# Softmax weights of 20 attention heads turned by VectorE and through DRAM instead of by TensorE

## The chip, the cores and the metric

One NeuronCore of a Trainium2 chip runs the whole program. The time is the device time of one execution in microseconds (us). The kernel before was timed in three runs: 898.75, 900.03 and 900.44 us, median 900.03 us.

## The reference, cut to what matters

A two-layer causal decoder trunk over 256 tokens of width 2048, in fp32. Each layer is a norm, one wide input projection, two kinds of attention heads, a SiLU gate, an output projection and the residual; a last norm follows.

```python
for i in range(DEPTH):                    # DEPTH = 2
    x = layer_even(x, norm0, w_in0, w_out0) if i % 2 == 0 else layer_odd(x, norm1, w_in1, b_f1, w_out1)
return rmsnorm(x, norm_f)
# layer_even: 10 heads "A" (an indexer picks 64 keys a query), 6 heads "B" (dilated windows)
# layer_odd:   8 heads "C" (stick-breaking, no softmax),        8 heads "D" (softmax with forget gates)
p = jax.nn.softmax(logits, axis=-1)       # A, B and D
o = jnp.einsum('bhqk,bkhd->bqhd', p, v)   # y = o * silu(gate); x + y @ w_out
```

## The kernel before, in words

**The projections.** TensorE's work is a chain of jobs (`jobs`, line 229): 14 of the first input projection (B0, K, I0, I1, B1, B2, B3, five pairs of A heads, B4, B5), four of its output projection (P0 to P3), 17 of layer two (C0, F1, G1, C2 to C7, D0 to D7) and four of the last output projection (Q0 to Q3). A job multiplies the 256 tokens (two tiles of 128) by a block of weights, mostly 512 columns wide, in 16 steps of 128 rows: *K steps*. Weights and activations are split into a high and a low fp32r part, so a K step is six matmuls (`products`, lines 320 to 326). F1 and G1 share the work of head C1 and are only 264 and 256 columns wide: the *narrow* jobs.

**The weights' way.** A weight *piece* is four K steps (1 MB for 512 columns). SyncE's queue (SP) issues its load into one of three `raw` tiles (`load`, line 256). ScalarE copies it in two halves to `whi` (line 282), VectorE subtracts to get `wlo` (line 283). Both have four buffers; `split` runs three halves ahead of the matmuls. A load overwrites the tile of the piece three before it, so SP waits for that piece's `wlo`.

**The order.** Every engine works through its instructions in the order in which the program writes them. `tick` (line 307) counts one tick for each K step of 512 columns (half a tick for a narrow one). Work beside the projections stands in generators: `yield n` puts what follows n ticks further on. A job is thus 16 ticks. When all of a piece is split, `split` starts `later(load, 4)` (line 287): the next load is issued four ticks on.

**A softmax head.** After its projection, `softmax_head` (line 540; heads B and D) or `heads_a` (line 723; two A heads) has queries and keys turned, multiplies them (`soft`, line 512: matmuls into `s`, exponentials into the tile `sn`, 128 x 384: 128 weights for the first 128 tokens and 256 for the second) and scales the weights (`share`, line 535). Then the weights must be turned, since the product with the values needs keys on partitions. `turn` (line 397) does this with three 128 x 128 TensorE transposes (line 400) into the PSUM tile `tp`; `cut` (line 465) reads `tp` into high and low parts; `weigh_out` (line 498) or its counterpart in `heads_a` multiplies by the values (`o`).

**The other way of turning** is in use already for queries, keys and gates (`qk`, `u`). `grid` (line 420) is one VectorE STREAM_TRANSPOSE, which turns each 32 x 32 block on its own into a tile `far`. `moved` (line 431) stores `far` to DRAM (`fard`, line 436) and reads it back so that the blocks land on their new partitions (line 438). What arrives is in block order with its rows permuted by `FAR` (line 52), and the host permutes the gate's weight columns to suit. Both transfers stand in SP's queue among the weight loads, and the reading waits until the store has landed. Gate values are turned this way by `gate_turned` (line 487), starting four ticks after the head.

Of the kernel before, what the change touches and what calls it, by code (L numbers as in the profile page):

```python
# [174 lines left out]
def trunk(ctx, tc, x, xT, g1, w0, wo0, w1, wo1, bf, gf, consts, rope, out):  # L175
# [243 lines left out]

    def grid(srcs):  # L420

        t = hp.tile([P, 512], F32, name="far", tag="rt2")
# [64 lines left out]
    def gate_turned(u, n=NT):  # L487
        uT = hp.tile([P, P * n], F32, name="uT", tag="uT" if n == NT else "rl")
        start(far([u], uT, 4, 2, 4))
        return arrived(uT, n)  # L490

    def gate_turned_here(u):
        pt = turn([u[:, 0:P], u[:, P:SEQ]])
        uT = hp.tile([P, SEQ], F32, name="uT", tag="uT")
        nc.scalar.activation(uT, pt[:, 0:SEQ], AF.Copy)
        return quarters(uT)

    def weigh_out(ph, pl, p1, v, uT, kt, swap):

        vh, vl, v1 = v  # L500
# [38 lines left out]

    def softmax_head(qk, ticks, nb, v, u, rs, kt, last):  # L540
        uT = None if last else gate_turned(u)
# [73 lines left out]
    def head_b(ps, h):  # L615
# [16 lines left out]
        if not last:  # L632
            start(far([qk], qk, 2, 2, 4))
        yield from softmax_head(qk, 12, bmask, v, u, hr0, YPOS[f"B{h}"], last)

# [22 lines left out]
    def index(ps, c):  # L658
        qr = [hp.tile([P, 512], F32, name="iqr", tag="qk") for _ in range(NT)]

        ih = hp.tile([P, 2, 512], F32R, name="ih", tag="ih", bufs=1)
        il = hp.tile([P, 4, 2, P], F32R, name="il", tag="il", bufs=1)
        for th in range(NT):
# [3 lines left out]
        yield 12  # L667
        hi, lo = (quarters(ih[:, j]) for j in range(2))
        nc.scalar.activation(hi, arrived(qr[0], 4), AF.Copy)
# [3 lines left out]
        d = [slice(0, DI), slice(DI, P)]  # L673
        two = lambda j: il[:, :, j].rearrange("p a (i c) -> p a i c", i=4)
        for j in range(2):
# [4 lines left out]
        for h2 in range(4):  # L680
            for th, s in BLK:
                n = P * (th + 1)
                pS = pa.tile([P, 512], F32, name="s", tag="s", bufs=1)
                if th == 0:
                    a = slice(h2 * P, (h2 + 1) * P)
                    three(pS[:, 0:SEQ], ih[:, 0, a], ih[:, 1, a], ikh[:, SEQ:512], ikl[:, SEQ:512])
                else:
                    for j in range(2):
                        o = pS[:, j * SEQ:(j + 1) * SEQ]
                        nc.tensor.matmul(o, il[:, h2, j], ikh[:, 0:SEQ], start=True, stop=False)  # L690
                        nc.tensor.matmul(o, il[:, h2, j], ikl[:, 0:SEQ], start=False, stop=True)
                rl = hp.tile([P, 512], F32, name="rl", tag="rl")
# [30 lines left out]
    def heads_a(ps, h):  # L723
# [22 lines left out]
        js = [slice(j * P, (j + 1) * P) for j in range(2)]  # L746

        ph, pl = (hp.tile([P, 2, SEQ], F32R, name="pA" + n, tag="i" + n, bufs=1) for n in "hl")
        p1h, p1l = (hp.tile([P, 2 * P], F32R, name="pB" + n, tag=t, bufs=1) for n, t in (("h", "y"), ("l", "sp")))

        def turned(j, pr):
            pt = turn([pr[:, 0:P], pr[:, P:SEQ], pr[:, SEQ:384]])
            cut((ph[:, j, :], pl[:, j, :]), pt[:, 0:SEQ])
            cut((p1h[:, js[j]], p1l[:, js[j]]), pt[:, SEQ:384])
# [10 lines left out]
        yield 3  # L765
        po = pa.tile([P, 512], F32, name="o", tag="o", bufs=1)
        vh, vl = vAs
# [19 lines left out]
    def gains_in(c):  # L787
        gb.append(hp.tile([P, 1024], F32, name="gb", tag=("ih", "il")[c], bufs=1))
        yield 12
        nc.gpsimd.dma_start(gb[c], gf[:, c * 1024:(c + 1) * 1024])  # L790

    def gain(c):

        yield (1, 1, 5)[c]
        for th in range(NT):
            s = xs[:, th, c * 512:(c + 1) * 512]
            nc.gpsimd.tensor_tensor(s, s, gb[c // 2][:, (c % 2) * 512:(c % 2 + 1) * 512], op=OP.mult)

# [138 lines left out]
    def head_d(ps, h):  # L937
# [4 lines left out]
        v, u = yield from vg1(ps, 256)  # L942
        yield from softmax_head(qk, 10, lambda: biases[h], v, u, None, HC + h, last)


    def tail(ps, c2):
# [7 lines left out]
        else:  # L954
            nc.vector.tensor_tensor(s, s, gb[1][:, 512:768], op=OP.mult)

    def finish(ps, th):
        if th == 0:
            residual(ps, 2, 3, (th,))
            norm(2, slice(0, 1))  # L960
            nc.gpsimd.tensor_tensor(xs[:, 0, 1536:1792], xs[:, 0, 1536:1792], gb[1][:, 512:768], op=OP.mult)

# [8 lines left out]
        nc.sync.dma_start(dst(0, 512), cols(0, 512))  # L971
        nc.vector.scalar_tensor_tensor(cols(1792, 2048), cols(1792, 2048), r, gb[1][:, 768:1024], op0=OP.mult,
                                       op1=OP.mult)
# [22 lines left out]
    for ji, (_, _, name, _) in enumerate(jobs):  # L996
# [18 lines left out]
        if name in ("D2", "D4"):  # L1015
            start(gains_in(len(gb)))
        if name == "B0":
# [59 lines left out]
```

## Time and profile before

| | |
|---|---|
| Median of three runs | 900.03 us (898.75 to 900.44) |
| Profiled execution, own time | 900.81 us |
| Its span, first to last instruction | 899.0 us |
| TensorE matmul busy | 888.9 us, 99% |
| VectorE / ScalarE / GpSimd busy | 72% / 53% / 6% |
| SP's DMA queue (q1) | 60.7% of the 16 DMA engines' span |
| Mean granted TensorE clock | 0.998 of full speed (2.4 GHz) |

Matmuls are pipelined: a row of the timeline shows when a matmul starts and how long it takes, and the starts of neighbours lie closer together than that. What a group of matmuls costs is therefore read from the starts around it. "SPq" is SP's queue; its rows are the issues of DMAs. In square brackets stands how long the engine was idle before a row, and what ended that.

### The profile page before, as it was taken

Reading aid. Unit: us, or ns where it says so; the run is one execution under the profiler, and the core shown is the slowest. Engines: PE = TensorE matmul, PEld = TensorE weight load, DVE = VectorE, ACT = ScalarE, POOL = GpSimd, SP = SyncE. Lnnn points to the kernel's source line nnn. Section 1 sums busy time; section 2 is a strip of 40 time slices with the busy share of each in tenths; the row PEclk is TensorE's granted clock in tenths of the full one; section 3 lists DMA queues with packets and bytes.
Section 4 is the critical chain, followed back from the end, with each engine's and each line's share of the span. In section 5 each row is a group of like instructions: output and inputs, shape, how many; then the busy total and the mean of one; then the engine's idle time right before and its main releaser. Section 6 shows DMA issues by size and latency. Waiting matters only on the chain.

```text
span 899.0 us, 11923 instructions
## 1 busy us (share of the span) xinstructions
PE 888.9 (99%) x4277; PEld 744.9 (83%) x4277; DVE 649.6 (72%) x1143; ACT 474.6 (53%) x833; POOL 50.1 (6%) x69
## 2 busy tenths in 40 slices
PE   9999999999999999999999999999999999999996
PEld 6988888888888888888897888888888888888886
DVE  7677888876777776666657777777787777776563
ACT  7654554454555455555445555555555555555440
POOL 0022100000000000000000000000000000001110
PEclk9999999999999999999999999999999999999999
DMA  9886655665565665666585665566676666655542
GB/s 357 324 318 235 212 199 195 209 241 193 202 213 195 216 222 186 236 234 234 159 276 204 229 211 200 201 208 202 220 256 226 239 217 213 207 202 186 191 184 94
DMA packets 70043, 196.56 MB, mean 219 GB/s; under 512 B 15568, under 2 KB 40672, under 8 KB 52064
## 3 DMA queue, kind: packets, MB, share of 16 engines
q1 hardware_dynamic: 68544, 192.50, 60.7%
q0 software_dynamic: 864, 2.12, 1.1%
q10 hardware_dynamic: 576, 1.19, 0.4%
q8 instruction: 33, 0.54, 0.3%
q14 instruction: 26, 0.21, 0.1%
HBM read 179.79 MB, written 16.00 MB: 218 GB/s over the span
## 4 chain that ended last, share of the span: by engine, by line
PE 93%; DMA 2%; issue 2%; DVE 2%; ACT 1%; POOL 0%; POOLq 0%; DVEq 0%; SPq 0%; ACTq 0%
PE pj L323 29%; PE pj L326 29%; PE pj L324 29%; DMA raw<-in_w_in_dram 1%; PE tp L400 1%; DVE wlo L283 1%; DMA w0yh<-in_w_in_dram 1%; PE s L516 1%; PE o L503 1%; PE s L455 1%; PE s L454 1%; PE s L456 1%; PE o L454 0%; PE o L456 0%; PE o L455 0%
## 5 line engine op out<-in xcount | busy, mean ns | idle before, releaser
L283 DVE TENSOR_TENSOR wlo<-raw,whi 128x1024 fp32r<-128x1024 f32 (+3 forms) x300 | 352.6, 1194 | 142.7 <-ACT whi L282 141.8
L323 PE MATMUL pj<-whi,xh 128*128 128x512 f32 (+3 forms) x992 | 380.4, 385 | 1.4 <-ACT whi L282 1.4
L324 PE MATMUL pj<-whi,xl 128*128 128x512 f32 (+3 forms) x992 | 376.4, 381 | 0.0
L282 ACT ACTIVATE whi<-raw 128x1024 fp32r<-128x1024 f32 (+3 forms) x300 | 298.6, 1023 | 83.2 <-PE pj L324 68.9
L326 PE MATMUL pj<-wlo,xh 128*128 128x512 f32 (+3 forms) x992 | 297.1, 381 | 0.2
L323 PEld LDWEIGHTS pj<-whi,xh 128*128 128x128 f32 x992 | 186.6, 188 | 35.1 <-ACT whi L282 3.1
L326 PEld LDWEIGHTS pj<-wlo,xh 128*128 128x128 f32 x992 | 183.2, 188 | 37.6 <-DVE wlo L283 1.9
L324 PEld LDWEIGHTS pj<-whi,xl 128*128 128x128 f32 x992 | 186.6, 188 | 32.2
L323 PE MATMUL pj<-whi,yh 128*128 128x512 f32 (+1 forms) x248 | 95.8, 386 | 0.0
L324 PE MATMUL pj<-whi,yl 128*128 128x512 f32 (+1 forms) x248 | 94.9, 383 | 0.0
L326 PE MATMUL pj<-wlo,yh 128*128 128x512 f32 (+1 forms) x248 | 76.7, 382 | 0.0
L326 PEld LDWEIGHTS pj<-wlo,yh 128*128 128x128 f32 x248 | 46.6, 188 | 9.3
L524 ACT ACTIVATE sn<-sn,nm 128x128 f32<-128x128 f32 (+1 forms) x48 | 21.5, 449 | 61.8 <-DVE nm L522 61.8
L324 PEld LDWEIGHTS pj<-whi,yl 128*128 128x128 f32 x248 | 46.6, 188 | 8.7
L323 PEld LDWEIGHTS pj<-whi,yh 128*128 128x128 f32 x248 | 46.6, 188 | 8.7
L467 ACT ACTIVATE yh<-uT 128x256 fp32r<-128x256 f32 (+1 forms) x27 | 12.4, 458 | 54.8 <-DVE uT L509 26.5
L561 ACT ACTIVATE sq<-xs 128x512 f32<-128x512 f32 x23 | 14.3, 623 | 28.5 <-DVE xs L784 26.6
L845 DVE RECIPROCAL e<-e 128x256 f32<-128x256 f32 x16 | 28.1, 1753 | 0.5
L382 POOL TENSOR_TENSOR qk<-rot,rot 128x256 f32<-128x256 f32 x16 | 11.8, 739 | 230.6 <-ACT sn L524 111.9
L468 DVE TENSOR_TENSOR yl<-uT,yh 128x256 fp32r<-128x256 f32 (+1 forms) x27 | 12.8, 475 | 14.3 <-ACT yh L467 14.3
L915 ACT ACTIVATE z<-z 128x384 f32<-128x384 f32 x8 | 4.2, 525 | 29.1 <-DVE z L914 29.1
L882 POOL DMA_DIRECT2D cb<-cTd x8 | 5.8, 720 | 246.2 <-DVE nb L887 221.7
(228 smaller groups left out, 737.3 us busy)
## 6 DMA issues: line engine op xcount, KB each, us to landing
raw<-in_w_in_dram SPq DMA_DIRECT2D x108, 1024.0 KB, 5.7
raw<-in_w_out_dram SPq DMA_DIRECT2D x32, 1024.0 KB, 4.8
fard<-far SPq DMA_DIRECT2D x43, 256.0 KB, 2.1
qk<-fard SPq DMA_DIRECT2D x25, 256.0 KB, 5.2
raw<-in_w_in_dram SPq DMA_DIRECT2D x4, 672.0 KB, 9.0
fard<-far SPq DMA_DIRECT2D x20, 128.0 KB, 3.7
uT<-fard SPq DMA_DIRECT2D x20, 128.0 KB, 5.1
raw<-in_w_in_dram SPq DMA_DIRECT2D x4, 528.0 KB, 3.9
```

The source lines that it names most:

```text
L282: nc.scalar.activation(hi, rw, AF.Copy)
L283: nc.vector.tensor_tensor(lo, rw, hi.bitcast(F32), op=OP.subtract)
L323: nc.tensor.matmul(o, a, wh, start=(kt == 0), stop=False)
L324: nc.tensor.matmul(o, b, wh, start=False, stop=False)
L326: nc.tensor.matmul(o, a, wl, start=False, stop=(kt == KT - 1))
L382: nc.gpsimd.tensor_tensor(dst, t1[:, 0:n], t2[:, 0:n], op=OP.add)
L400: nc.tensor.transpose(pt[:, i * P:(i + 1) * P], s, ident)
L467: nc.scalar.activation(dst[0], src, AF.Copy)
L468: nc.vector.tensor_tensor(dst[1], src, dst[0].bitcast(F32), op=OP.subtract)
L524: nc.scalar.activation(sn[:, s], sn[:, s], AF.Exp, scale=-1.0, bias=nm[:, th:th + 1], accum_out=l[:, th:th + 1])
L561: nc.scalar.activation(j, xs[:, th, c * 512:(c + 1) * 512], AF.Square, accum_out=ss[:, i, th, c:c + 1])
L845: nc.vector.reciprocal(e, e)
```

## The change

- `softmax_head` and `heads_a` send the scaled weights of 20 heads (B0 to B3, all ten A heads, D0 to D5) through `grid` and `moved` instead of `turn`; B4, B5, D6 and D7 (`near`) keep the TensorE transposes. The store is two ticks after `grid`, the reading four after that, `cut` four after the reading in all of them (for heads B and D `cut` was four ticks after `share` in all; for A one tick after the second `share`).
- `moved` gets `ordered`: four readings of 32 partitions each, in place of one of 128, which put the keys back in natural order, in place into `sn`.
- Gate values are turned eight ticks after the head instead of four.
- After a piece of a narrow job the next load is two ticks on instead of four.
- The two loads of x in three column parts each become two loads.
- To free tiles, `ih`, `il` and the gains `gb` are cut in halves with tags of their own; the second A head's `far` lies in one of them. The gains come in four DMAs instead of two.

```diff
             for th in range(NT):
-                for c0, c1 in ((0, 768), (768, 1536), (1536, D)):
-                    nc.sync.dma_start(xs[:, th, c0:c1], x[th * P:(th + 1) * P, c0:c1])
+                nc.sync.dma_start(xs[:, th, :], x[th * P:(th + 1) * P, :])
...
-                load() if ji == 0 else start(later(load, 4))
+                load() if ji == 0 else start(later(load, 2 if w < 300 else 4))
...
-    def moved(t, dst, done, stored):
+    def moved(t, dst, done, stored, ordered=False):
...
         yield done
         nc.sync.dma_start(d, t)
         yield stored
+        if ordered:
+            w = P * n // 4
+            for j in range(4):
+                nc.sync.dma_start(dst[32 * j:32 * j + 32].rearrange("p (i f) -> p i f", i=4),
+                                  d[:, j * w:(j + 1) * w].rearrange("(i l) f -> l i f", i=4))
+            return
...
     def gate_turned(u, n=NT):
-        uT = hp.tile([P, P * n], F32, name="uT", tag="uT" if n == NT else "rl")
-        start(far([u], uT, 4, 2, 4))
-        return arrived(uT, n)
+        box = []
+        def way():
+            yield 8
+            t = grid([u])
+            uT = hp.tile([P, P * n], F32, name="uT", tag="uT" if n == NT else "rl")
+            yield from moved(t, uT, 2, 4)
+            box.append(arrived(uT, n))
+        start(way())
+        return box
...
-    def softmax_head(qk, ticks, nb, v, u, rs, kt, last):
+    def softmax_head(qk, ticks, nb, v, u, rs, kt, last, near):
...
         share(pr, factor(l, rs))
-        yield 4
-        pt = turn([pr[:, 0:P], pr[:, P:SEQ], pr[:, SEQ:384]])
+        if near:
+            yield 4
+            blocks = quarters(turn([pr[:, 0:P], pr[:, P:SEQ], pr[:, SEQ:384]]))
+        else:
+            yield from moved(grid([pr]), pr, 2, 4, True)
+            yield 4
+            blocks = arrived(pr, 3)
...
-        cut((ph, pl), pt[:, 0:SEQ])
-        nc.scalar.activation(p1, pt[:, SEQ:384], AF.Copy)
+        cut((quarters(ph), quarters(pl)), blocks[:, 0:2])
+        nc.scalar.activation(quarters(p1), blocks[:, 2:3], AF.Copy)
...
         def turned(j, pr):
-            pt = turn([pr[:, 0:P], pr[:, P:SEQ], pr[:, SEQ:384]])
+            pt = arrived(pr, 3)
...
             share(sm[j][0], factor(sm[j][1], hr0))
-        yield 1
+            t = hp.tile([P, 512], F32, name="far", tag="ih2", bufs=1) if j else None
+            start(moved(grid([sm[j][0]], t), sm[j][0], 2, 4, True))
+        yield 8
...
         turned(0, sm[0][0])
-        yield 3
+        yield 2
         turned(1, sm[1][0])
```

**TensorE, the first A pair's weights.** Before, the first A head's three transposes stand between two K steps of the next job (`pj` are the two token tiles' sums; line 400 is `turn`):

```order
L326 MATMUL pj_2129<-wlo,xh 128x512
L326 MATMUL pj_2130<-wlo,xh 128x512
L400 MATMUL tp<-cons,sn 128x128 x3
L323 MATMUL pj_2129<-whi,xh 128x512
L324 MATMUL pj_2129<-whi,xl 128x512
```

Now no transposes stand there; the pair's product with the values (`o`) has moved from behind the 11th K step of the next job to behind the first K step of the job after that:

```order
L462 MATMUL s<-kAh,qql 128x256
L322 MATMUL pj_2375<-whi,xh 128x512
L323 MATMUL pj_2375<-whi,xl 128x512
L322 MATMUL pj_2376<-whi,xh 128x512
L323 MATMUL pj_2376<-whi,xl 128x512
L325 MATMUL pj_2375<-wlo,xh 128x512
L325 MATMUL pj_2376<-wlo,xh 128x512
L460 MATMUL o<-pAh,vAh 128x512
```

The six matmuls of `o` are unchanged in number; 20 groups of three transposes are gone from the engine.

**SP, one job of the A stretch.** Before (256 is a weight load, 436 a store, 438 a reading):

```order
L436 DMA fard<-far 128x512
L256 DMA raw<-in_w_in_dram 128x2048
L436 DMA fard<-far 128x512
L438 DMA qk<-fard 128x4x128
L256 DMA raw<-in_w_in_dram 128x2048
L438 DMA uT<-fard 128x4x128
L256 DMA raw<-in_w_in_dram 128x2048 x2
```

Now (441 is one of the four readings, 444 the old kind):

```order
L436 DMA fard<-far 128x512
L256 DMA raw<-in_w_in_dram 128x2048
L436 DMA fard<-far 128x384 x2
L444 DMA qk<-fard 128x4x128
L441 DMA sn<-fard 32x4x96 x4
L256 DMA raw<-in_w_in_dram 128x2048
L436 DMA fard<-far 128x512
L441 DMA sn<-fard 32x4x96 x4
L256 DMA raw<-in_w_in_dram 128x2048
L444 DMA uT<-fard 128x4x128
L256 DMA raw<-in_w_in_dram 128x2048
```

Ahead of the job's second load now stand two stores and five readings (a store and a reading before), ahead of the third a store and four readings (a reading before).

**SP, around the narrow jobs.** Before, from the loads for G1 (1024 wide) to the first two for C2 (2048):

```order
L256 DMA raw<-in_w_in_dram 128x1024
L436 DMA fard<-far 128x256
L256 DMA raw<-in_w_in_dram 128x1024 x2
L436 DMA fard<-far 128x512
L438 DMA uT<-fard 128x4x64
L256 DMA raw<-in_w_in_dram 128x2048
L438 DMA qk<-fard 128x4x128
L256 DMA raw<-in_w_in_dram 128x2048 x4
```

Now:

```order
L256 DMA raw<-in_w_in_dram 128x1024 x2
L444 DMA qk<-fard 128x4x128
L256 DMA raw<-in_w_in_dram 128x1024 x2
L436 DMA fard<-far 128x512
L256 DMA raw<-in_w_in_dram 128x2048
L436 DMA fard<-far 128x256
L256 DMA raw<-in_w_in_dram 128x2048
L444 DMA qk<-fard 128x4x128
L256 DMA raw<-in_w_in_dram 128x2048
```

The store of C0's gate values (128x256) no longer stands ahead of G1's last two loads nor of C2's first, and the gate's reading no longer ahead of C2's first.

## Rows read from the trace of the kernel before

**Rows 1.** The page, busy time of each engine (us, share of the span, instructions).

```profile
PE 888.9 (99%) x4277; PEld 744.9 (83%) x4277; DVE 649.6 (72%) x1143; ACT 474.6 (53%) x833; POOL 50.1 (6%) x69
```

**Rows 2.** Stretches: length, busy PE, PEld, DVE, ACT, POOL, clock, DMA share, GB/s.

```profile
100.00:150.00 50.00, 50.00 (x241) 41.83 (x241) 42.59 (x90) 26.51 (x44) 2.96 (x4) 1.00 0.55 194
250.00:300.00 50.00, 50.00 (x240) 41.72 (x239) 37.61 (x79) 25.96 (x51) 2.95 (x4) 1.00 0.63 215
450.00:500.00 50.00, 48.67 (x290) 41.78 (x289) 33.28 (x57) 26.24 (x49) 2.01 (x3) 1.00 0.69 239
```

**Rows 3.** TensorE's transposes of softmax weights by form: count, busy us, mean ns, idle before.

```profile
L400 PE MATMUL tp<-cons,sn 128*128 128x128 f32 x72 | 11.7, 271 | 0.0
```

**Rows 4.** TensorE's timeline around two of these turns: start, us, row.

```profile
64.97 0.39 PE L323 MATMUL pj<-whi,xh 128*128 128x512 f32 x1
...
66.33 0.49 PE L400 MATMUL tp<-cons,sn 128*128 128x128 f32 x3
66.58 0.48 PE L323 MATMUL pj<-whi,xh 128*128 128x512 f32 x1
...
68.05 0.39 PE L323 MATMUL pj<-whi,xh 128*128 128x512 f32 x1
...
736.26 0.49 PE L400 MATMUL tp<-cons,sn 128*128 128x128 f32 x3
...
737.98 0.39 PE L323 MATMUL pj<-whi,xh 128*128 128x512 f32 x1
```

**Rows 5.** Timeline from C0's end to C2's first half, four engines.

```profile
454.65 0.44 DVE L428 STREAM_TRANSPOSE far<-u 128x256 f32<-128x256 f32 x1
...
455.12 0.33 SPq L436 DMA_DIRECT2D fard<-far  x1
455.54 0.89 SPq L256 DMA_DIRECT2D raw<-in_w_in_dram  x2
458.20 0.33 SPq L436 DMA_DIRECT2D fard<-far  x1
...
459.10 0.61 SPq L256 DMA_DIRECT2D raw<-in_w_in_dram  x1
...
467.01 1.06 ACT L282 ACTIVATE whi<-raw 128x1024 fp32r<-128x1024 f32 x1 [4.43 <-DMA raw<-in_w_in_dram]
...
472.47 0.50 PE L323 MATMUL pj<-whi,xh 128*128 128x512 f32 x1 [0.96 <-ACT whi L282]
```

**Rows 6.** VectorE's transposes of queries and keys by form (as rows 3).

```profile
L428 DVE STREAM_TRANSPOSE far<-qk 128x512 f32<-128x512 f32 x25 | 17.7, 709 | 0.5
```

**Rows 7.** SP's queue in one job of the A stretch.

```profile
240.69 0.38 SPq L256 DMA_DIRECT2D raw<-in_w_in_dram  x1
...
244.43 0.38 SPq L438 DMA_DIRECT2D qk<-fard  x1
245.11 0.33 SPq L256 DMA_DIRECT2D raw<-in_w_in_dram  x1
...
250.81 5.56 SPq L256 DMA_DIRECT2D raw<-in_w_in_dram  x2
```

**Rows 8.** DMA issues: tile, count, KB each, median us to landing.

```profile
raw<-in_w_in_dram SPq DMA_DIRECT2D x108, 1024.0 KB, 5.7
...
qk<-fard SPq DMA_DIRECT2D x25, 256.0 KB, 5.2
...
fard<-far SPq DMA_DIRECT2D x20, 128.0 KB, 3.7
uT<-fard SPq DMA_DIRECT2D x20, 128.0 KB, 5.1
...
uT<-fard SPq DMA_DIRECT2D x5, 256.0 KB, 7.1
```

**Rows 9.** ScalarE's copies of the pieces loaded at 240.69 and 245.11.

```profile
253.71 2.24 ACT L282 ACTIVATE whi<-raw 128x1024 fp32r<-128x1024 f32 x2
```

More of the change, by code (lines that the diff above doesn't have):

```diff
@@ L418, in arrived, with grid @@
         return t.rearrange("p (i b c) -> p b i c", i=4, b=n)
-    def grid(srcs):
-        t = hp.tile([P, 512], F32, name="far", tag="rt2")
+    def grid(srcs, t=None):
+        t = hp.tile([P, 512], F32, name="far", tag="rt2") if t is None else t
         ns = [x.shape[1] // P for x in srcs]
@@ L495, in gate_turned_here @@
         nc.scalar.activation(uT, pt[:, 0:SEQ], AF.Copy)
-        return quarters(uT)
+        return [quarters(uT)]
     def weigh_out(ph, pl, p1, v, uT, kt, swap):
+        uT, = uT
         vh, vl, v1 = v
@@ L633, in head_b @@
             start(far([qk], qk, 2, 2, 4))
-        yield from softmax_head(qk, 12, bmask, v, u, hr0, YPOS[f"B{h}"], last)
+        yield from softmax_head(qk, 12, bmask, v, u, hr0, YPOS[f"B{h}"], last, h >= HB - 2)
     def keys_a(ps):
@@ L659, in index @@
         qr = [hp.tile([P, 512], F32, name="iqr", tag="qk") for _ in range(NT)]
-        ih = hp.tile([P, 2, 512], F32R, name="ih", tag="ih", bufs=1)
-        il = hp.tile([P, 4, 2, P], F32R, name="il", tag="il", bufs=1)
+        ih = [hp.tile([P, 512], F32R, name="ih", tag=t, bufs=1) for t in ("ih", "ih2")]
+        il = [hp.tile([P, 4, P], F32R, name="il", tag=t, bufs=1) for t in ("il", "il2")]
         for th in range(NT):
@@ L667, in index @@
         yield 12
-        hi, lo = (quarters(ih[:, j]) for j in range(2))
+        hi, lo = (quarters(t) for t in ih)
         nc.scalar.activation(hi, arrived(qr[0], 4), AF.Copy)
@@ L673, in index @@
         d = [slice(0, DI), slice(DI, P)]
-        two = lambda j: il[:, :, j].rearrange("p a (i c) -> p a i c", i=4)
+        two = lambda j: il[j].rearrange("p a (i c) -> p a i c", i=4)
         for j in range(2):
@@ L685, in index @@
                     a = slice(h2 * P, (h2 + 1) * P)
-                    three(pS[:, 0:SEQ], ih[:, 0, a], ih[:, 1, a], ikh[:, SEQ:512], ikl[:, SEQ:512])
+                    three(pS[:, 0:SEQ], ih[0][:, a], ih[1][:, a], ikh[:, SEQ:512], ikl[:, SEQ:512])
                 else:
@@ L689, in index @@
                         o = pS[:, j * SEQ:(j + 1) * SEQ]
-                        nc.tensor.matmul(o, il[:, h2, j], ikh[:, 0:SEQ], start=True, stop=False)
-                        nc.tensor.matmul(o, il[:, h2, j], ikl[:, 0:SEQ], start=False, stop=True)
+                        nc.tensor.matmul(o, il[j][:, h2], ikh[:, 0:SEQ], start=True, stop=False)
+                        nc.tensor.matmul(o, il[j][:, h2], ikl[:, 0:SEQ], start=False, stop=True)
                 rl = hp.tile([P, 512], F32, name="rl", tag="rl")
@@ L746, in heads_a @@
         js = [slice(j * P, (j + 1) * P) for j in range(2)]
-        ph, pl = (hp.tile([P, 2, SEQ], F32R, name="pA" + n, tag="i" + n, bufs=1) for n in "hl")
-        p1h, p1l = (hp.tile([P, 2 * P], F32R, name="pB" + n, tag=t, bufs=1) for n, t in (("h", "y"), ("l", "sp")))
         def turned(j, pr):
-            pt = turn([pr[:, 0:P], pr[:, P:SEQ], pr[:, SEQ:384]])
-            cut((ph[:, j, :], pl[:, j, :]), pt[:, 0:SEQ])
-            cut((p1h[:, js[j]], p1l[:, js[j]]), pt[:, SEQ:384])
+            pt = arrived(pr, 3)
+            cut((quarters(ph[:, j, :]), quarters(pl[:, j, :])), pt[:, 0:2])
+            cut((quarters(p1h[:, js[j]]), quarters(p1l[:, js[j]])), pt[:, 2:3])
         sm = []
@@ L760, in heads_a @@
             share(sm[j][0], factor(sm[j][1], hr0))
-        yield 1
+            t = hp.tile([P, 512], F32, name="far", tag="ih2", bufs=1) if j else None
+            start(moved(grid([sm[j][0]], t), sm[j][0], 2, 4, True))
+        yield 8
+        ph, pl = (hp.tile([P, 2, SEQ], F32R, name="pA" + n, tag="i" + n, bufs=1) for n in "hl")
+        p1h, p1l = (hp.tile([P, 2 * P], F32R, name="pB" + n, tag=t, bufs=1) for n, t in (("h", "y"), ("l", "sp")))
         turned(0, sm[0][0])
-        yield 3
+        yield 2
         turned(1, sm[1][0])
         yield 3
+        uT, = uT
         po = pa.tile([P, 512], F32, name="o", tag="o", bufs=1)
@@ L787, in gains_in @@
     def gains_in(c):
-        gb.append(hp.tile([P, 1024], F32, name="gb", tag=("ih", "il")[c], bufs=1))
+        gb.append(hp.tile([P, 512], F32, name="gb", tag=("ih", "ih2", "il", "il2")[c], bufs=1))
         yield 12
-        nc.gpsimd.dma_start(gb[c], gf[:, c * 1024:(c + 1) * 1024])
+        nc.gpsimd.dma_start(gb[c], gf[:, c * 512:(c + 1) * 512])
     def gain(c):
@@ L796, in gain @@
             s = xs[:, th, c * 512:(c + 1) * 512]
-            nc.gpsimd.tensor_tensor(s, s, gb[c // 2][:, (c % 2) * 512:(c % 2 + 1) * 512], op=OP.mult)
+            nc.gpsimd.tensor_tensor(s, s, gb[c], op=OP.mult)
     def feed1(ps, c):
@@ L942, in head_d @@
         v, u = yield from vg1(ps, 256)
-        yield from softmax_head(qk, 10, lambda: biases[h], v, u, None, HC + h, last)
+        yield from softmax_head(qk, 10, lambda: biases[h], v, u, None, HC + h, last, h >= HDD - 2)
     def tail(ps, c2):
@@ L954, in tail @@
         else:
-            nc.vector.tensor_tensor(s, s, gb[1][:, 512:768], op=OP.mult)
+            nc.vector.tensor_tensor(s, s, gb[3][:, 0:256], op=OP.mult)
     def finish(ps, th):
@@ L960, in finish @@
             norm(2, slice(0, 1))
-            nc.gpsimd.tensor_tensor(xs[:, 0, 1536:1792], xs[:, 0, 1536:1792], gb[1][:, 512:768], op=OP.mult)
+            nc.gpsimd.tensor_tensor(xs[:, 0, 1536:1792], xs[:, 0, 1536:1792], gb[3][:, 0:256], op=OP.mult)
             nc.vector.tensor_reduce(ssp[:, 0:1], ss[:, 2, 1, 0:3], axis=mybir.AxisListType.X, op=OP.add)
@@ L971, in finish @@
         nc.sync.dma_start(dst(0, 512), cols(0, 512))
-        nc.vector.scalar_tensor_tensor(cols(1792, 2048), cols(1792, 2048), r, gb[1][:, 768:1024], op0=OP.mult,
+        nc.vector.scalar_tensor_tensor(cols(1792, 2048), cols(1792, 2048), r, gb[3][:, 256:512], op0=OP.mult,
                                        op1=OP.mult)
@@ L1015, in trunk @@
         if name in ("D2", "D4"):
-            start(gains_in(len(gb)))
+            for _ in range(2):
+                start(gains_in(len(gb)))
         if name == "B0":
```

## The prediction

> **What bounds the kernel now.** I read the busy times first. TensorE is busy for 99% of the span, VectorE for 72% [rows 1]. Since a busy TensorE need not be the bound everywhere, I then read stretches: in the stretch of the B heads and the indexer, and in that of the A heads, it is busy for 50.00 of 50 us; only around the narrow jobs does it drop, to 48.67 [rows 2]. So matmuls are the path nearly everywhere: what leaves TensorE's queue there shortens the run by its spacing in that queue, as long as no operand comes later than now. The one place with time to gain otherwise is 450 to 500 us. The timelines say what a turn costs and what the queues have to spare.
>
> **Taking the turns off TensorE.** 72 transposes of weights are 24 groups of three [rows 3]; 20 groups go. Before B0's group a K step takes 66.33 - 64.97 = 1.36 us. From the group's start to the second K step behind it, it is 68.05 - 66.33 = 1.72 us, so group and K step cost 0.36 us more than a K step alone. Of that, 0.25 us (66.58 - 66.33) is the group, and 0.11 us is the K step behind it running slower. A D head's group gives 737.98 - 736.26 = 1.72 us again [rows 4]. 20 x 0.36 = 7.2 us, all on the path, since TensorE has no idle time beside these groups. If the slow K step came from something else, 20 x 0.25 = 5.0 us would be left: the lower end. The matmuls with the values only change places.
>
> The VectorE page of the Trainium skill ("VectorE: DVE Perf Modes", Rules for kernel authors) speaks against this part: a 128 x 128 transpose belongs on TensorE if PSUM will do as its destination. By that rule the 7.2 us would not be had; the rows decide for the engine with time to spare, and the rule returns below as a rival.
>
> **What VectorE gets.** One STREAM_TRANSPOSE of 128 x 384 a head. No such form is in the trace; 128 x 256 takes 0.44 us [rows 5] and 128 x 512 takes 0.71 us [rows 6], so I take 0.57 us, midway (an estimate), 11.4 us for 20. A job lasts 23 to 25 us here and brings one or two, so at most some 2.4 us come into 50 us. VectorE is idle for 50 - 42.59 = 7.4 us in the densest stretch and 12.4 us among the A heads [rows 2]. That idle time covers it: nothing on the path. Without cover it would be the whole 11.4 us. `cut` still takes as many instructions on ScalarE and VectorE; its source is `sn` instead of PSUM. I count no change.
>
> **What SP's queue gets.** A store (0.33 us to issue [rows 5]) and four readings (0.38 each [rows 7]) a head: 1.85 us, 37 us over 20 heads. They also stand ahead of weight loads, and each reading waits until its store has landed. The A stretch is the hard place, with two heads a job. There the second load of the job was issued at 245.11, behind the reading at 244.43 [rows 7]. ScalarE first reads that piece with the second of the two copies that begin at 253.71, so at about 254.9 [rows 9]. A load lands 5.7 us after its issue [rows 8], so it can be late by 254.9 - 245.1 - 5.7 = 4.1 us before even ScalarE notices. Ahead of it now stand one store more, and four readings: 0.33 + 4 x 0.38 = 1.85 us. The landing of the first head's store lies under that, because the store of the second head waits for `share` and `grid` of that head anyway. The third load (250.81) gets a store and four readings ahead of it in place of a reading, 1.5 us more, and its piece is needed some 10 us after the second one's. In B and D jobs the readings come in between two loads four ticks, about 5.4 us, apart. I take zero for late loads. Behind ScalarE's notice stand the three halves that `split` runs ahead, so TensorE would be later still.
>
> **When the weights arrive.** `cut` stands four ticks, 5.4 us, behind the readings' place. Four readings of 48 KB are not in the trace. The nearest rows are the gates' readings: 128 KB lands after 5.1 us, 256 KB after 7.1 us, the latter beside more traffic [rows 8]. Lower bound: a 128 KB store, 3.7 us [rows 8]. The last of four is issued 1.1 us behind the first. SP usually reaches them before their tick, because it waits for VectorE and not for TensorE. I take 5.1 us, nearest in pieces and direction: on time, or late by under 1 us, which ScalarE bears, because the product with the values is three ticks (4.1 us) further on and `cut` needs about 1.5 us of them (four instructions, which I estimate at the 0.44 us of the 128 x 256 form [rows 5] or less).
>
> Half the bytes land no sooner: 128 KB of gates take 5.1 us and 256 KB of queries 5.2 us [rows 8]. The DMA page of the Trainium skill ("DMA: Bandwidth & Descriptors", Rules for kernel authors) goes further and speaks against this part: many small transfers should be made into one, since under 64 KB one pays mostly overhead. By that rule four readings cost up to four times that overhead; run side by side they leave the sum as it is, and one after the other they are rival 1.
>
> **DMA traffic.** 20 x (192 + 192) KB come to 7.9 MB. At one A job twice 384 KB come to four loads of 1024 KB and four transfers of 256 KB, 15%: the DMA share of 0.63 [rows 2] becomes 0.73 by bytes, and still under 0.8 if small pieces cost double. The loads keep pace.
>
> **The narrow jobs.** C2's first load is issued at 459.10 and read by ScalarE only at 467.01, after 4.43 us of waiting; TensorE then waits for 0.96 us at 472.47 [rows 5]. The load stood behind two things: the store of C0's gate, which waited for VectorE until 455.1 and held G1's last loads (455.54), so that these were still in flight; and the gate's reading. With loads two ticks on and the gate turned later, G1's loads go out early and C2's first stands right behind the store at 458.20, 0.5 us sooner, on a free DMA queue. At 5.7 us to landing it is there by about 464.3, before TensorE wants it. What can be had is 1.33 us (50 - 48.67), the least is zero or, if the gate's store now holds C2's second load, another wait of the same 1 us. I take 1.0 us.
>
> **Edits at nothing.** x in two loads instead of six: the same bytes in the same place of the queue, with four issues fewer. The halves `ih`, `il`, `gb`: the same instructions on other tiles, two more DMAs on GpSimd, which is 6% busy [rows 1].
>
> **Sum.** 900.8 (the profiled execution's own time) - 7.2 - 1.0 = 892.6 us. The median of the runs is 0.8 us below that execution, so I predict **891.8 us**.
>
> **The rivals.**
> 1. *Weights back late, part of the gain lost.* If the four readings land one after the other, at 7.1 us for the last and 1.1 us of issue, `cut` is 2.8 us late, and of the 4.1 us to the product 1.5 us are used: 0.2 us over. 20 x 0.2 us is 4 us given back: 896. For it: the reading waits behind a store in SP. Against: the same path serves queries with the same four ticks, and TensorE has no gap from it.
> 2. *Slower: late weight loads among the A heads.* Should SP wait for each store in full (3.7 us) before its readings, both heads of a pair cost 2 x (3.7 + 1.85) = 11.1 us of queue a job, 5.6 us for each of two loads. From 4.1 us on they are late to ScalarE; once the halves ahead are used up, ten loads x 1.5 us = 15 us, minus 8.2: 907. Against: stores and readings are interleaved so that most landings are over.
> 3. *Slower: VectorE becomes the bound.* The rule of the VectorE page above would be right if VectorE set the pace: 11.4 us more on it, 8.2 us gained: 903. Decides where its idle time falls under the added 2.4 us in 50; it has 7.4 at the least [rows 2].
> 4. *Nothing comes of it.* The time of the turns is lost again in waits for weights, as the loads set the pace: 900. Against: TensorE waits for no load outside the narrow jobs.
>
> **How the numbers follow.** Forecast 0.78, rival 1 0.12, rival 2 0.04, rival 3 0.03, rival 4 0.03. The forecast's own range goes from 890.4 (8.2 us and the rest of the 1.33 us, and 0.05 us more a turn) to 894.0 (5.0 us and 1.0). With rival 1 the range reaches from 890.2 to 896.0; left out are mainly rivals 2 to 4. A measurement of this kernel can tell about 0.2%, 1.8 us, from no change: faster 0.90, same 0.04, slower 0.06.
>
> **What would show it.** Right: three transposes of `sn` left in each of four groups (12, not 72); the start of the job after an A job 0.7 us sooner than now; TensorE at 50.0 of 50 in the A stretch and over 49.5 around the narrow jobs; readings of `sn` landing within 5 to 6 us; ScalarE's waits for them small. Wrong: TensorE waiting for `ph`, `pAl` or `whi` among A heads, waits of ScalarE for `raw` there, or VectorE at over 48 of 50 us.

## The result and the profile after

The changed kernel takes 908.93 us (median of 4 runs, 908.28 to 909.32) where the kernel before took 899.39 us beside it: a ratio of 1.0098, interval 1.0082 to 1.0115. It is slower by some 9 us; the forecast was 8 us faster. The profiled execution spans 907.4 us.

Busy times of the page (PEld: TensorE's weight loads, which overlap its matmuls), against [rows 1]:

```profile
PE 888.5 (98%) x4217; PEld 741.4 (82%) x4217; DVE 658.2 (73%) x1163; ACT 476.0 (52%) x833; POOL 50.5 (6%) x71
```

TensorE has 60 instructions fewer and VectorE 20 more, as the change says. The stretches of [rows 2], and one more (length, busy PE, PEld, DVE, ACT, POOL, clock, DMA share, GB/s):

```profile
100.00:150.00 50.00, 50.00 (x240) 41.86 (x239) 42.50 (x90) 27.72 (x45) 2.96 (x4) 1.00 0.55 192
250.00:300.00 50.00, 45.25 (x203) 35.17 (x201) 33.42 (x74) 22.90 (x48) 2.95 (x4) 1.00 0.61 209
300.00:350.00 50.00, 45.78 (x193) 36.70 (x193) 34.22 (x73) 22.86 (x47) 3.21 (x6) 0.93 0.66 230
450.00:500.00 50.00, 49.56 (x316) 44.42 (x315) 33.00 (x57) 25.50 (x50) 0.00 (x0) 1.00 0.63 216
```

The B stretch is as full as before, the narrow jobs are fuller (49.56 for 48.67), and the A heads, which were at 50.00 of 50, lose 4.8 and 4.2 us in two stretches. Two single instructions mark the stages: VectorE's first `u` of an A head stands behind the first A job's matmuls, and the first `xs<-pj,xs` behind the first job after the attention. The times at the end of a row are its first and last start. Before:

```profile
L732 DVE SCALAR_TENSOR_TENSOR u<-tg,pj x10: 409/414/417, 188.2 to 286.0; 128x256 f32<-128x256 f32 x10
L784 DVE TENSOR_TENSOR xs<-pj,xs x15: 680/686/692, 357.6 to 880.5; 128x512 f32<-128x512 f32 x15
```

After:

```profile
L754 DVE SCALAR_TENSOR_TENSOR u<-tg,pj x10: 410/414/416, 187.3 to 291.6; 128x256 f32<-128x256 f32 x10
L808 DVE TENSOR_TENSOR xs<-pj,xs x15: 680/684/692, 370.0 to 888.9; 128x512 f32<-128x512 f32 x15
```

Up to the first A head: 188.2 before, 187.3 after, 0.9 us gained. The A stretch, from there to the first `xs`: 357.6 - 188.2 = 169.4 before, 370.0 - 187.3 = 182.7 after, **13.3 us lost**. From there to the end of the span: 541.4 before, 537.4 after, 4.0 us gained. So the gains outside the A heads came, and the A heads, from which 3.6 us were forecast as gain, lost 13.3.

What TensorE and ScalarE wait for between 200 and 345 us (engine, line, releaser: us in total, times, longest):

```profile
ACT pAh L473 <- DMA sn<-fard: 32.5, 10, 4.0
...
PEld o L460 <- ACT pAh L473: 9.4, 4, 2.8
PE o L460 <- ACT pAh L473: 7.7, 4, 2.4
...
ACT whi L281 <- DMA raw<-in_w_in_dram: 2.3, 1, 2.3
```

The first cut of each of the ten A heads waits for its weights, 3.3 us on average, and TensorE then waits for four of these cuts. SP's queue in one A job, against [rows 7]:

```profile
242.39 0.32 SPq L436 DMA_DIRECT2D fard<-far  x1
242.80 0.38 SPq L256 DMA_DIRECT2D raw<-in_w_in_dram  x1
243.24 3.26 SPq L436 DMA_DIRECT2D fard<-far  x2
246.60 0.38 SPq L444 DMA_DIRECT2D qk<-fard  x1
248.84 1.75 SPq L441 DMA_DIRECT2D sn<-fard  x4
250.71 0.36 SPq L256 DMA_DIRECT2D raw<-in_w_in_dram  x1
251.11 0.43 SPq L436 DMA_DIRECT2D fard<-far  x1
251.59 2.53 SPq L441 DMA_DIRECT2D sn<-fard  x4
```

The second head's last reading is issued by 254.1. What lies around it, from the chain of work that ended last in this stretch (start, us, what); the row with brackets is ScalarE's own, with its idle time:

```profile
244.99 0.56 DVE sn L554 x2
...
253.70 4.44 DMA sn<-fard
...
258.24 0.42 ACT L473 ACTIVATE pAh<-sn 128x256 fp32r<-128x256 f32 x1 [3.98 <-DMA sn<-fard]
258.24 0.09 ACT pAh L473
...
258.85 0.96 ACT whi L281
...
259.84 1.23 DVE wlo L282
261.06 0.20 DVE sn L538
...
265.41 0.61 DVE uT L796
...
266.04 0.64 ACT yh L473
...
266.70 0.69 DVE yl L474
...
267.70 0.56 DVE sn L554 x2
...
268.36 0.34 DVE far L427
```

The second head's `share` is at 244.99. Its last reading lands at 258.14, 13.2 us later; ScalarE had stood at the cut since 254.26, 9.3 us after that `share`. The late cut runs (`pAh`, at 258.24), and behind it in ScalarE's and VectorE's order stand the next pieces of weights and the **next pair's** softmax (L538) and `share` (L554); the grid for the next store is at 268.36. With the store, its landing and the readings the chain comes back to the cut. From one pair's first store to the next is 27.7 us here; before it was 24.8 us (240.27 to 265.02), with TensorE full, so now TensorE waits. This was my theory for the experiments: a loop through the way back.

The transfers (tile, count, KB each, median us from issue to landing), against [rows 8]:

```profile
raw<-in_w_in_dram SPq DMA_DIRECT2D x108, 1024.0 KB, 5.6
...
fard<-far SPq DMA_DIRECT2D x20, 192.0 KB, 2.9
sn<-fard SPq DMA_DIRECT2D x80, 48.0 KB, 4.6
```

### The profile page after: what moved, and what is told of

Its sections match the earlier page's. It is cut to its first block, busy times and chain, and to the rows that moved or that the text cites. A ratio compares the mean times of both kernels' runs of the same rounds, so it can differ in the third digit from the quotient of the medians.

```text
span 907.4 us, 12037 instructions
## 1 busy us (share of the span) xinstructions
PE 888.5 (98%) x4217; PEld 741.4 (82%) x4217; DVE 658.2 (73%) x1163; ACT 476.0 (52%) x833; POOL 50.5 (6%) x71
## 4 chain that ended last, share of the span: by engine, by line
PE 80%; DVE 6%; DMA 5%; ACT 3%; issue 2%; SPq 2%; POOL 0%; DVEq 0%; POOLq 0%; ACTq 0%
PE pj L322 25%; PE pj L323 25%; PE pj L325 25%; DVE wlo L282 3%; DMA sn<-fard 2%; DMA fard<-far 2%; SPq L441 2%; ACT whi L281 1%; ACT sn L540 1%; DMA w0yh<-in_w_in_dram 1%; PE o L519 1%; DVE sn L554 0%; DVE far L427 0%; PE s L461 0%; PE s L462 0%
## 5 line engine op out<-in xcount | busy, mean ns | idle before, releaser
L281 ACT ACTIVATE whi<-raw 128x1024 fp32r<-128x1024 f32 (+3 forms) x300 | 298.1, 1024 | 115.3 <-PE pj L323 82.7
L473 ACT ACTIVATE pAh<-sn 128x256 fp32r<-128x256 f32 x10 | 4.2, 417 | 32.5 <-DMA sn<-fard 32.5
L474 DVE TENSOR_TENSOR pAl<-sn,pAh 128x256 fp32r<-128x256 f32 x10 | 4.3, 425 | 22.7 <-ACT pAh L473 22.7
```

The costliest lines, as they stand in the source:

```text
L473: nc.scalar.activation(dst[0], src, AF.Copy)
L474: nc.vector.tensor_tensor(dst[1], src, dst[0].bitcast(F32), op=OP.subtract)
```

## The experiments

All are timed beside the kernel before. "A stretch" is worked out as above: 169.4 before, 182.7 after.

| run | edit, from the changed kernel | us | ratio, 95% interval | A stretch |
|---|---|---|---|---|
| a_near | A heads turned on TensorE | 895.47 | 0.9952 [0.9938, 0.9967] | 169.1 |
| only_a | B and D heads turned on TensorE | 911.63 | 1.0130 [1.0115, 1.0145] | 182.8 |
| a_one | one reading a head in A (leaves the keys in another order) | 903.05 | 1.0034 [1.0022, 1.0045] | 176.1 |
| a_pool | A's readings on GpSimd | 924.42 | 1.0271 [1.0256, 1.0287] | 197.7 |
| a_late | A's cuts three ticks later | 901.64 | 1.0017 [1.0008, 1.0027] | 174.9 |
| a_half | only the first head of a pair | 897.58 | 0.9973 [0.9964, 0.9982] | 169.7 |
| a_gate4 | gate of A at 4 ticks again | 909.61 | 1.0108 [1.0094, 1.0122] | 182.6 |
| before_narrow | kernel before, narrow loads alone | 899.35 | 0.9993 [0.9984, 1.0002] | 169.4 |
| a_la2 | A's loads at 2 ticks | 905.93 | 1.0068 [1.0054, 1.0083] | 179.1 |
| a_late_la2 | a_late, A's loads at 2 ticks | 899.24 | 0.9999 [0.9988, 1.0009] | 173.7 |
| a_late_la1 | a_late, A's loads at 1 tick | 902.12 | 1.0028 [1.0012, 1.0044] | 174.6 |
| a_late_one | a_late and a_one (keys again in another order) | 902.25 | 1.0022 [1.0013, 1.0031] | 175.7 |
| a_hold | a_late_la2, second store later | 899.88 | 0.9989 [0.9976, 1.0001] | 172.9 |
| a_dead | a_near, transfers kept, unused | 895.44 | 0.9940 [0.9918, 0.9962] | 169.1 |
| a_late_pool_rs | a_late, A's stores and readings on GpSimd | 894.13 | 0.9930 [0.9907, 0.9953] | 165.7 |
| a_pool_rs | the same queue, cuts not later | 917.95 | 1.0197 [1.0179, 1.0214] | 190.5 |
| best | a_late_pool_rs again | 895.14 | 0.9936 [0.9920, 0.9951] | 167.8 |

### Which heads lose: a_near, only_a

```diff
# a_near, in heads_a
-            pt = arrived(pr, 3)
+            pt = turn([pr[:, 0:P], pr[:, P:SEQ], pr[:, SEQ:384]])
...
-            t = hp.tile([P, 512], F32, name="far", tag="ih2", bufs=1) if j else None
-            start(moved(grid([sm[j][0]], t), sm[j][0], 2, 4, True))
-        yield 8
+        yield 1
# only_a, in head_b and head_d
-..., last, h >= HB - 2)
+..., last, True)
```

> The changed kernel, but the five pairs of A heads turn their weights on TensorE again, as in the kernel before; the ten B and D heads keep the way through DRAM. Theory: the way back of the A heads' weights is a loop (share, grid, store, four readings a head behind each other in SP's queue, landing, cut, then the next pair's soft) that is longer than the pair's matmuls; it costs some 3.7 us in each of 5 pairs, while B and D heads gain 0.36 us a turn. Then this kernel has the gains alone: 10 x 0.36 + 0.9 of the narrow jobs = 4.5 under the kernel before, about 895 us, and the pair's period is back at some 24.7 us. Rival one (all the added transfers are too much beside the weight loads, B and D as well): about half of the loss stays, 903 or more. Rival two (the loss is from another edit in the A jobs, such as the gate's store at 8 ticks): 905 or more.

> The changed kernel, but the ten B and D heads turn their weights on TensorE again; only the A heads go through DRAM. Theory of the A heads' loop: the loss stays whole and the ten turns come back, 908.9 + 10 x 0.36 = 912.5 us. Rival one (too many transfers everywhere): the loss shrinks with the transfers, about 904 us.

Both came within 1 us of what the theory gave, and rival one and rival two fell. The A heads lose everything; the ten B and D heads and the narrow jobs give 4.6 us.

### What in the way back: a_one, a_pool, a_gate4

```diff
# a_one
-            start(moved(grid([sm[j][0]], t), sm[j][0], 2, 4, True))
+            start(moved(grid([sm[j][0]], t), sm[j][0], 2, 4))
# a_pool, in moved (its new argument q is nc.sync unless given) and in heads_a
-                nc.sync.dma_start(dst[32 * j:32 * j + 32]...
+                q.dma_start(dst[32 * j:32 * j + 32]...
...
-            start(moved(grid([sm[j][0]], t), sm[j][0], 2, 4, True))
+            start(moved(grid([sm[j][0]], t), sm[j][0], 2, 4, True, nc.gpsimd))
# a_gate4, in gate_turned
-            yield 8
+            yield 8 if n == NT else 4
```

> The changed kernel, but in the A heads each head's weights come back in one reading of 192 KB in place of four of 48 KB. This leaves the key rows of the A heads' weights in another order than the values, so the A heads' output is another one; number and size of all other instructions stay. If the loop is long because eight readings are issued one after another in SP's queue (6 fewer of some 0.43 us each in a pair), the pair gets 2.6 us shorter: 5 x 2.6 = 13 under the changed kernel, about 896 us. If the time is in the landing of store and reading (5.2 and 4.4 us) or in DMA bandwidth, little changes: 906 to 909 us.

> The changed kernel, but the A heads' readings are issued from GpSimd's queue, which is idle there, in place of SP's. If the wait is for SP (the readings stand behind the qk reading, a weight load and the gate's store, and hold up the second weight load), the pair's period falls by up to 3 us and the whole is about 897 us. If the landing itself is the cost, or GpSimd issues as slowly, 906 to 910 us.

> The changed kernel, but in the A jobs alone the gate's blocks are turned and stored four ticks earlier again, as in the kernel before, so that the gate's store no longer stands between the two heads' readings in SP's queue. If that place in the queue is a main part of the loss (the store waits for its semaphore lane and for VectorE's grid there), 3 us or more come back: under 906 us. If the loop is made by the order of cut and soft and by the landings, this moves little: 907 to 910 us.

One reading gave back 5.9 us of the 13 expected: eight issues are a part of the loop, not the whole. GpSimd's queue made it 15.5 us worse, outside both values expected. It issues no slower by much (0.55 us a reading), but its readings land later (7.3 us in the median, last row; 4.6 in the changed kernel). If they lengthen the loop once in each of five pairs, these 2.7 us make 13.5 us (an estimate); the A stretch grew by 15.0. TensorE also had a lower clock in this run (0.93 granted from 187 to 372 us, for 0.98 over the changed kernel's A stretch); what share that has was not separated.

```profile
sn<-fard SPq DMA_DIRECT2D x40, 48.0 KB, 5.0
sn<-fard POOLq DMA_DIRECT2D x40, 48.0 KB, 7.3
```

The gate's place in SP's queue makes no difference (909.61 for 908.93).

### Opening the loop: a_late, a_half

```diff
# a_late, in heads_a
-        yield 8
+        yield 11
 
         ph, pl = ...
# a_half
-            pt = arrived(pr, 3)
+            pt = quarters(turn(...)) if j == 1 else arrived(pr, 3)
...
+            if j != 1:
+                start(moved(grid([sm[j][0]]), sm[j][0], 2, 4, True))
```

> The changed kernel, but the A heads' two cuts and the product with the values stand three ticks (some 4.5 us) further on in the program, so that the second head's cut comes behind the next pair's first soft on ScalarE and VectorE; transfers, their order and their queues are as in the changed kernel. If the loss is the loop in which a cut that waits for its reading holds up the next pair's soft, three ticks more than cover the 3.7 us of a pair: the pair is back at 24 us, and the whole comes near the forecast, about 893 us (892 to 897). If the loss is in the transfers themselves (SP held up so that weight loads come late, DMA bandwidth), it stays: 905 to 909 us.

> The changed kernel, but of each A pair only the first head's weights go through DRAM; the second head's are turned on TensorE. If the loop closes over the second head (the readings of which are issued and land last), this takes away half of the transfers and the last link: 5 turns of 0.36 us are given back, and the whole is about 894 us, a little under the 895.5 of the kernel whose A heads are all turned on TensorE. If each way through DRAM costs its own part of the loss (four readings and a store of SP's time), half of the loss stays: about 902 us.

Both fell between the theories. Later cuts gave back 7.3 us, about half of what the A heads cost; a_half, 897.6, is 2 us worse than no A head at all through DRAM, not 2 us better. So the theory was half of it. In a_late ScalarE no longer waits for the weights' readings but for the load of a piece that TensorE needs, and for the queries:

```profile
ACT whi L281 <- DMA raw<-in_w_in_dram: 17.5, 4, 5.6
...
ACT qqh L764 <- DMA qk<-fard: 5.0, 3, 2.0
```

In its SP queue the two stores are at 240.31 to 245.56 (the second waits for VectorE's grid), then come the queries' reading, four readings, and only at 248.19 the second load, which lands 7.73 us later; `whi` starts on it at 256.02, after 5.6 us of waiting.

```profile
240.31 5.25 SPq L436 DMA_DIRECT2D fard<-far  x2
245.66 0.38 SPq L444 DMA_DIRECT2D qk<-fard  x1
246.13 1.94 SPq L441 DMA_DIRECT2D sn<-fard  x4
248.19 0.36 SPq L256 DMA_DIRECT2D raw<-in_w_in_dram  x1
```

From there the chain of this run goes on through the next pair's first softmax (`sn` at 259.42) to the grid of its second head and that head's store, behind which the next second load stands, at 275.42:

```profile
256.02 1.07 ACT whi L281
...
259.42 0.99 ACT sn L540 x4
...
271.90 0.59 DVE far L427
272.50 0.32 SPq L436
```

So this is a second loop of the same kind, closed over a weight load: the copy `whi` that waits for it stands ahead of the next pair's softmax on ScalarE. From one second load to the next is 27.2 us. In each of the five pairs ScalarE waits for such a load, 3.7 to 5.6 us.

### Reordering SP's queue: a_late_la2, a_late_la1, a_late_one, a_la2, a_hold

```diff
# la2 (la1: 1 for A)
-start(later(load, 2 if w < 300 else 4))
+start(later(load, 2 if w < 300 else 2 if jobs[ji][2][0] == "A" else 4))
# a_hold: a_late_la2 and
-            start(moved(grid([sm[j][0]], t), sm[j][0], 2, 4, True))
+            start(moved(grid([sm[j][0]], t), sm[j][0], 5 if j else 2, 4, True))
```

> The kernel with the later cuts (901.6), and in the A jobs the weight loads start two ticks on in place of four, so that a pair's second load stands in SP's queue ahead of the qk reading and the first head's four readings. In the kernel with the later cuts ScalarE still waits up to 5.6 us for a weight load that was issued behind those readings. If that is the second half of the loss, some 7 us come back: about 894 us (892 to 897), as good as the kernel whose A heads are turned on TensorE or better. If the loads are late through bandwidth and not through the queue, no gain: 900 to 903 us.

> As the run before it, with the A jobs' loads one tick on: the second load stands ahead of the second head's store, and the third ahead of the second head's readings. If late loads are the rest of the loss, 892 to 896 us, no worse than two ticks; if SP then waits for the buffers that the loads fill and holds up the readings by it, 898 us or more.

> The kernel with the later cuts, and in the A heads one reading of 192 KB a head in place of four of 48 KB (keys in another order than the values, so the A heads' output is another one). With the loop gone and six of the eight issues gone from SP's queue, nothing of either cause should be left: about 894 us. If the rest of the loss is bandwidth, 900 to 902 us as in the kernel with the later cuts.

> The changed kernel (908.9), with only the A jobs' weight loads two ticks on; cuts where the change has them. If the order of cut and soft closes the loop first, as the waits of the changed kernel say, this alone gives little: 905 to 909 us, while it gives some 7 us once the cuts are later. If late loads alone were the cause, about 896 to 900 us.

> The kernel with the later cuts, the A jobs' loads two ticks on, and the second head's store held back three ticks more, so that in SP's queue a pair's second load, the qk reading and the first head's readings stand ahead of that store, which waits for VectorE. If the rest of the loss is that SP is held by this store while loads and qk reading stand behind it, 893 to 897 us. If holding it only makes the second head's weights late instead, 899 us or more.

None gave what was hoped; the best, a_late_la2, is 2.4 us under a_late. With the loads two ticks on, ScalarE's wait for them fell from 17.5 to 4.3 us, and the queries, now behind the load, took its place (a_late_la2):

```profile
ACT qqh L764 <- DMA qk<-fard: 16.4, 4, 5.5
...
ACT whi L281 <- DMA raw<-in_w_in_dram: 4.3, 1, 4.3
```

In a_hold that wait is 16.1 us. So no order of SP's queue that I tried was free: whatever stands behind the stores and readings is late. And six issues fewer (a_late_one) gave nothing once the cuts were later, so issue time is not what is short. a_la2 says that the loads alone are a small part as long as the cuts are early, as expected.

### Transfers without their latency, and the other queue: a_dead, a_late_pool_rs, a_pool_rs, best

```diff
# a_dead: a_near, and behind share (the weights are turned on TensorE before the readings overwrite them)
+            t = hp.tile([P, 512], F32, name="far", tag="ih2", bufs=1) if j else None
+            start(moved(grid([sm[j][0]], t), sm[j][0], 2, 4, True))
# a_late_pool_rs and best: a_late, and in moved (its new arguments qs and qr are nc.sync unless given) and in heads_a;
# a_pool_rs: the same without a_late
-        nc.sync.dma_start(d, t)
+        qs.dma_start(d, t)
...
-                nc.sync.dma_start(dst[32 * j:32 * j + 32]...
+                qr.dma_start(dst[32 * j:32 * j + 32]...
...
-            start(moved(grid([sm[j][0]], t), sm[j][0], 2, 4, True))
+            start(moved(grid([sm[j][0]], t), sm[j][0], 2, 4, True, nc.gpsimd, nc.gpsimd))
```

> The kernel whose A heads are turned on TensorE (895.5), but the A heads' grids, stores and readings of the changed kernel are issued too, at the same places of SP's and VectorE's order; the readings write the weights once more into a buffer that nobody reads after TensorE has turned it. If the loss comes only from what waits for the way back (cut, and with it the next pair's soft), the transfers cost next to nothing: 895 to 897 us. If the transfers in SP's queue make weight loads and qk readings late by themselves, the 6 us of loss that later cuts left show here as well: 900 to 903 us.

> The kernel with the later cuts (901.6), but the A heads' stores and readings are both issued from GpSimd's queue, so that SP's queue in the A jobs holds only what it holds in the kernel before. If SP's queue makes the rest of the loss, it goes: 893 to 897 us. If the weights are still back too late (a reading from GpSimd took 7.3 us to land, 4.6 from SP), or VectorE's and ScalarE's order is the rest, 900 us or more.

> The changed kernel (cuts where the change has them), with the A heads' stores and readings both issued from GpSimd's queue. If the cut that waits for its readings and stands ahead of the next pair's soft closes a loop by itself, the loss stays: 903 us or more. If SP's queue alone made the loss, it is gone without any later cut: 893 to 897 us.

> The kernel with later cuts and the A heads' stores and readings on GpSimd's queue once more, against the kernel before: 894.1 +- 1 us, 0.993 of it. The forecast for the change as it was written was 891.8.

a_dead is the plainest of all: the same 10 grids, 10 stores and 40 readings in the same places of SP's queue cost nothing (895.44 against 895.47 without them) as long as nobody waits for them. Traffic, issue time and VectorE's extra work are therefore not the loss by themselves. a_late_pool_rs loses nothing: TensorE is full in the A stretch of both (a_dead first, then a_late_pool_rs, columns as above).

```profile
250.00:300.00 50.00, 50.00 (x240) 41.69 (x239) 39.80 (x84) 25.25 (x50) 2.96 (x4) 1.00 0.74 243
250.00:300.00 50.00, 50.00 (x234) 41.83 (x233) 38.94 (x83) 26.53 (x51) 13.98 (x24) 1.00 0.76 256
```

In a_late_pool_rs GpSimd stores a pair's second head at 244.16, the next pair's two heads at 261.23 and 268.17, and the second head of the pair after it at 292.17: 24.0 us a pair.

```profile
244.16 0.56 POOL L436 DMA_DIRECT2D fard<-far  x1 [6.36 <-DVE far L427]
244.79 4.37 POOL L441 DMA_DIRECT2D sn<-fard  x8
...
261.23 0.58 POOL L436 DMA_DIRECT2D fard<-far  x1 [3.46 <-DVE nm L538]
268.17 0.56 POOL L436 DMA_DIRECT2D fard<-far  x1 [6.37 <-DVE far L427]
...
292.17 0.56 POOL L436 DMA_DIRECT2D fard<-far  x1 [6.36 <-DVE far L427]
```

The two by two of queue and cuts: cuts early, 908.9 on SP and 918.0 on GpSimd; cuts later, 901.6 and 894.1 (895.1 again). Neither edit alone is enough, and the other queue alone does harm.

## Why the prediction was wrong

- **The turns leave TensorE: right; the 0.36 us each only in part.** 12 transposes of `sn` are left (first and last start in the row). In the trace of a_late_pool_rs the A stretch is 169.4 - 165.7 = 3.7 us shorter for ten turns, as forecast. In its second trace, best, it is only 1.6 us shorter, with ScalarE waiting 15.2 us in all for weight loads (4.6 in the first), so the room in it is small. Giving the ten B and D turns back to TensorE (only_a) cost 911.63 - 908.93 = 2.7 us, 0.27 each. As a whole these kernels are 6.2 and 5.3 us under the kernel before, not 8.2.

```profile
L399 PE MATMUL tp<-cons,sn x12: 270/272/273, 353.1 to 825.1; 128*128 128x128 f32 x12
```

- **VectorE: right.** The 128 x 384 form took 579 ns, for the 0.57 us estimated; it stays hidden, also in a_dead. Rival 3 fell.

```profile
L427 DVE STREAM_TRANSPOSE far<-sn 128x384 f32<-128x384 f32 x20 | 11.6, 579 | 1.3
```

- **Traffic: right.** The DMA share in the A stretch of a_dead, with all the transfers, is 0.74 (forecast 0.73), and they cost nothing there.
- **When the weights arrive: the step that failed.** "On time, or late by under 1 us, which ScalarE bears." The landing itself was well sized (4.6 us for 5.1). But that SP would reach the readings before their tick was wrong for two heads at once (four ticks, 5.4 us, ahead of the place where ScalarE waited would be 248.9; the second head's were issued from 251.59 to 254.12), and so was counting the way from `share` to the cut in ticks of one head. The way also holds the store's issue and landing, the first head's readings ahead of the second's, and eight issues: 13.2 us in the pair above, where ScalarE stood at the cut after 9.3. The cut was late by 3.3 us on average. What turned that into a loss of 16.9 us (13.3 lost where 3.6 were to be gained) instead of rival 1's few is what I did not follow: behind the waiting cut on ScalarE and VectorE stand the next pair's softmax and `share`, from which the next way starts. A delay does not end in the slack before the product; it comes back in the next pair. In a D job, where only one head is under way, the same four readings closed no such loop: ScalarE waits for them there too, in all six D heads (and in none of the four B heads), but TensorE stays full (50.00 of 50 from 700 to 750 and from 750 to 800 us).

```profile
ACT ph L473 <- DMA sn<-fard: 17.1, 6, 3.7
```

- **SP's queue at zero for late loads: wrong once the cuts are later.** As the changed kernel stands it is small (2.3 us of waiting for `raw`). With later cuts it is what is left: loads or queries late by up to 5.6 us, and 6.2 us of the run (901.64 against a_near's 895.47). Rival 2 had the direction and, by luck, nearly the time (907): it held SP for landings, while the loss came from cuts.
- **The narrow jobs: about right.** 450 to 500 us is at 49.56, 0.9 us better, for 1.0. Alone (before_narrow, forecast 1.0) the edit gives 0.7 us, inside its interval, [0.9984, 1.0002], so its own size is not shown; in the trace of that run TensorE is at 50.00 of 50 there.
- **TensorE's clock does not make the loss.** In the four runs of the changed kernel its mean is 0.994 to 0.998, and the times, 908.28 to 909.32 us, do not follow it (908.28 at 0.994, 908.72 at 0.998).
- **What stays open.** The A jobs keep 6 us of loss on SP's queue with later cuts, while the same transfers are free in a_dead. The trace of a_late shows one loop that does it, over the second weight load, and taking stores and readings out of that queue ends it. But with that load moved ahead (a_late_la2) the queries' reading is late in its place; why each order tried on SP's queue keeps a loss once the cuts need the readings was not separated further.
- **Two figures of the forecast do not add up**, with no weight in the outcome: the range starts at 890.2 us where its own best case is 890.4, and rivals 2 and 3 together make 0.07 of "slower", not 0.06.

## What to carry to other kernels

A way through DRAM costs its latency where the program waits for it, not its transfers: before adding one, write down what stands behind the waiting instruction on its engine, and see whether the next round's start is among it. If so, put the wait behind that start, and give the transfers a queue in which no load stands behind a store that waits for an engine; here the two together gave 0.993 of the time before, and either alone was slower than before. An experiment that keeps all transfers and lets nobody wait for them tells the two costs apart in one run.

## What the runs showed of the hardware

The 48 KB readings landed after 4.6 us (median) from SP's queue in the changed kernel; those of the A heads landed after 6.0 us (a_late_pool_rs) to 7.3 us (a_pool) from GpSimd's, and each took 0.55 us of GpSimd. The DMA page of the Trainium skill ("DMA: Bandwidth & Descriptors", Rules for kernel authors) says that spreading transfers over SP, ScalarE and GpSimd does not help bandwidth and only saves issue time. No run here tests the bandwidth; what the other queue saved here was not issue time (a_late_one) but the waiting of the entries that stood behind it. The rule in the same table of the Trainium skill that one issues a transfer early and waits for it late is borne out by a_late, 7.3 us.

Merging four readings into one, the rule of the Trainium skill's DMA page that the prediction weighed, gave 5.9 us while the loop was closed and nothing (902.25 for 901.64) once the cuts were later.

TensorE's granted clock was 0.93 between 300 and 350 us of the changed kernel, so at 1.2 in place of 2.4 GHz for part of it, after a stretch in which it was idle for 4.75 of 50 us; in a_near, a_dead and a_late_pool_rs, which keep it full there, it is 1.00. Idle time did not lower it each time: in a_one it is 1.00 from 300 to 350 us with TensorE idle for 5.65 of 50 us.
